# The feed-forward's first product from half-size products: seven in place of eight

## The chip, the cores and the metric

One core of a Trainium2 chip runs the whole program. The metric is the device time of one execution in microseconds (us). A core has a matrix engine (TensorE, PE in the profile, its weight loads PEld), a vector engine (VectorE, DVE), an activation engine (ScalarE, ACT), a general engine (GpSimd, POOL) and SyncE (SP), whose queue starts the loads. Every engine works through its own instructions in order and waits on semaphores for the others.

## The reference

A decoder layer over 512 tokens of 1024 features: a mixer of three head groups, its output projection, then a gated feed-forward with 2816 inner features. In float32:

```
h = rmsnorm(x, pre_mix_g[l])
proj = h @ w_in[l]
...
mix = jnp.concatenate([a_out, b_out, c_out], axis=-1) @ w_out[l]
x = x + rmsnorm(mix, post_mix_g[l])
h = rmsnorm(x, pre_ffn_g[l])
gate, up = jnp.split(h @ w_ffn_in[l], 2, axis=-1)
f = (jax.nn.silu(gate) * up) @ w_ffn_out[l]
x = x + rmsnorm(f, post_ffn_g[l])
```

The change is in `h @ w_ffn_in`: 512 x 1024 times 1024 x 5632.

## The kernel before, in words

Every large product is made of float32r matmuls in two parts. A factor is split into a high part (a cast to float32r, ScalarE, L183) and a low part (the rest, `wl = wf - wh`, VectorE or GpSimd, L185), and a product is high times high, high times low and low times high: three matmuls in place of one. Weights come as tiles of 128 x 1024 float32 (512 KB) in two raw buffers (`wf`, loaded by SyncE in `w_load`, L156), and go split into four pairs of buffers (`wh`, `wl`). `Feed` hands them out in the order of use, at a high priority.

TensorE's order is written by hand: a class `Order` keeps a clock of TensorE's work, runs one main sequence and slots in side sequences when what they wait for should be there. The order on the other engines is set by a scheduler from priorities, and their queues are then fixed.

Stages: the input norm and projection with the three mixers beside it; the output projection (`tm_gemm`, tokens on the partitions, 512 columns at a time); the norm of its result, turned by TensorE so that features lie on the partitions (`turn`, L1142 to L1156: `h2` and `l2`, high and low part, 128 x 8 x 512); then the feed-forward's first product. It has 22 blocks of 128 inner features. A block takes two weight tiles, gate and up columns, and makes two PSUM banks (128 features x 512 tokens) with 24 matmuls each (`ffn_mm`: eight depth blocks by three matmuls). Blocks 0 and 1 run in two halves of 256 tokens, since the second half of the tokens is turned later; blocks 2 to 21 with 512 columns. After a block `gate` applies silu on ScalarE (L1177), multiplies on VectorE (L1178) and splits the result for the second product (L1179, L1180). Banks alternate: `acc` (two) for even blocks, `sb` (three) for odd ones. The second product (`tm_gemm` again, with `w_ffn_out`) and the last norm end the program.

Of the kernel before, what the change touches and what calls it, by code (L numbers as in the profile page):

```python
# [96 lines left out]
def block_kernel(ctx: ExitStack, tc: tile.TileContext, x, pre_mix_g, w_in, rwkv_mu, rwkv_w0, rwkv_w2,  # L97
# [924 lines left out]
    def pair_slice(k):  # L1022
        return slice(k[0], k[1] + 1, k[1] - k[0])
# [22 lines left out]
    for ui, unit in enumerate(o_units):  # L1046
        if ui == 2:
# [4 lines left out]
            grow = early.tile([128, D], F32, name="grow")  # L1052
            frow = early.tile([128, D], F32, name="frow")
# [12 lines left out]
    wsp2 = ph2.enter_context(tc.tile_pool(name="wsplit2", bufs=2, side="right"))  # L1066

# [1 line left out]
    res = ph2.enter_context(tc.tile_pool(name="res", bufs=1))  # L1069
    wpools = (wspool, wsp2)  # L1070
    h2 = res.tile([128, KB, S], F32R, name="h2")
    l2 = res.tile([128, KB, S], F32R, name="l2")
    sm = res.tile([128, 3 * NB], F32, name="sm")
# [64 lines left out]
    def turn(t):  # L1138
        """The normed input of the feed-forward, features on the partitions."""
# [10 lines left out]
        for i in range(2):  # L1150
# [4 lines left out]
            act.copy(h2[:, 4 * i:4 * i + 4, tk], p3)  # L1155
            dve.tensor_tensor(l2[:, 4 * i:4 * i + 4, tk], p3, h2[:, 4 * i:4 * i + 4, tk].bitcast(F32), op=OP.subtract)  # L1156
# [11 lines left out]
    FM = FB - KB  # L1168
    fhm = res.tile([128, FM, S], F32R, name="fhm")
    flm = res.tile([128, FM, S], F32R, name="flm")  # L1170
    fh = [fhm[:, i] if i < FM else mh[:, i - FM] for i in range(FB)]
    fl = [flm[:, i] if i < FM else ml[:, i - FM] for i in range(FB)]
    ffeed = Feed([(w_ffn_in[0], slice(0, 8), c + 128 * b, 128) for b in range(FB) for c in (0, FF)], wpools, on_pool=(1, 3))

    def gate(b, pg):
        f = res.tile([128, S], F32, name="etmp", bufs=2)
        act.activation(f, pg[0], AF.Silu)  # L1177
        dve.tensor_tensor(f, f, pg[1], op=OP.mult)  # L1178
        act.copy(fh[b], f)  # L1179
        dve.tensor_tensor(fl[b], f, fh[b].bitcast(F32), op=OP.subtract)  # L1180
# [11 lines left out]
    ws = [ffn_w() for _ in range(4)]  # L1192
# [5 lines left out]
    gate(0, pf[0:2])  # L1198
    gate(1, pf[2:4])
    for b in range(2, FB):  # L1200
        pg = []
        for i in range(2):
            p = (sb if b % 2 else acc)()
            ffn_mm(p, *ffn_w(), slice(0, S))
            pg.append(p)
        gate(b, pg)
# [40 lines left out]
```

## Time and profile before

| what | us |
|---|---|
| three runs, median (lowest to highest) | 704.51 (702.69 to 706.77) |
| the profiled execution: span, first to last instruction | 700.0 |
| the profiled execution: its own time | not listed apart from the three runs |
| TensorE busy in the span | 671.8 |
| VectorE busy | 335.0 |
| ScalarE busy | 253.7 |
| GpSimd busy | 132.7 |
| blocks 2 to 21 of the first product, 351.7 to 570.4 | 218.7 |
| second product and end, 570.4 to 700.0 | 129.6 |

The profile is one execution. Busy time counts an instruction from its start to its end; TensorE's matmuls overlap (a new one starts before the last has ended), so the pace is read from one start to the next. A note in brackets behind a row gives the idle time ahead of it and who ended it. `x3` behind a row means three such instructions in a row, with their time from the first's start to the last's end.

### The profile page before, as it was taken

What the parts mean: (1) busy time and instruction counts of PE and PEld (TensorE: products, weight loads), DVE (VectorE), ACT (ScalarE), POOL (GpSimd) and SP (SyncE); (2) the same over time, 40 slices, a digit from 0 to 9 for tenths busy, and PEclk for the clock granted to TensorE, in tenths of its full rate; (3) what the DMA queues carried; (4) which work ended last, traced back from release to release, by engine and by line L of the source; (5) the groups of instructions that cost most, each with busy time, mean ns of one, the idle gap of its engine ahead of it and who ended that gap; (6) DMA issues with size and microseconds to landing.
All of it is one profiled execution on the core that took longest, in us unless ns stands there. A gap on an engine that the chain in (4) does not pass through costs nothing.

```text
span 700.0 us, 9724 instructions
## 1 busy us (share of the span) xinstructions
PE 671.8 (96%) x3918; PEld 546.1 (78%) x3918; DVE 335.0 (48%) x588; ACT 253.7 (36%) x451; POOL 132.7 (19%) x149
## 2 busy tenths in 40 slices
PE   7998999799999997998999999999999999999996
PEld 6876878577777785777988888888888888888885
DVE  4688879935353566458442332323323232223214
ACT  6753443335455454336332322233222331122111
POOL 6272435522413226115000000000000000000001
PEclk9999999799999998999999999999999999999999
DMA  7322112211101117233243333333333332223203
GB/s 238 113 62 61 45 43 69 86 32 34 52 31 31 31 61 247 83 92 116 67 139 101 90 91 94 109 100 90 91 94 109 99 90 91 91 91 100 99 13 121
DMA packets 80286, 61.15 MB, mean 87 GB/s; under 512 B 2120, under 2 KB 70128, under 8 KB 80240
## 3 DMA queue, kind: packets, MB, share of 16 engines
q1 hardware_dynamic: 78192, 57.70, 26.9%
q10 hardware_dynamic: 2048, 2.82, 1.2%
q8 instruction: 31, 0.51, 0.3%
q14 instruction: 15, 0.12, 0.1%
HBM read 58.41 MB, written 2.10 MB: 86 GB/s over the span
## 4 chain that ended last, share of the span: by engine, by line
PE 50%; DVE 2%; issue 1%; ACT 1%; POOL 1%; DVEq 0%; POOLq 0%; ACTq 0%
PE sb L112 21%; PE acc L112 21%; PE yb L112 3%; PE rb L112 3%; PE ob L112 2%; DVE x L1129 1%; DVE xs L1146 1%; ACT raw L1142 1%; POOL rs L1126 0%; POOL ss L1144 0%; DVE etmp L1116 0%; ACT wdad L1110 0%; DVE wl L185 0%; DVEq L1243 0%; PE rb L117 0%
## 5 line engine op out<-in xcount | busy, mean ns | idle before, releaser
L183 ACT ACTIVATE wh<-wf 128x1024 fp32r<-128x1024 f32 (+2 forms) x120 | 104.1, 886 | 285.6 <-PE sb L112 123.1
L185 DVE TENSOR_TENSOR wl<-wf,wh 128x1024 fp32r<-128x1024 f32 (+1 forms) x76 | 89.4, 1180 | 170.9 <-ACT wh L183 168.6
L185 POOL TENSOR_TENSOR wl<-wf,wh 128x512 fp32r<-128x512 f32 (+2 forms) x44 | 71.3, 1639 | 111.5 <-ACT wh L183 72.1
L1126 POOL TENSOR_TENSOR rs<-rs,mhalf 128x1 f32<-128x1 f32 x8 | 6.2, 778 | 380.0 <-DVE rs L1121 376.8
L112 PE MATMUL acc<-l,wh 128*128 128x512 f32 (+1 forms) x192 | 72.5, 378 | 1.9 <-DVE l L1156 1.9
L112 PE MATMUL acc<-h,wh 128*128 128x512 f32 (+1 forms) x192 | 72.2, 376 | 0.0
L112 PE MATMUL acc<-h,wl 128*128 128x512 f32 (+1 forms) x192 | 71.9, 374 | 0.0
L112 PE MATMUL sb<-l,wh 128*128 128x512 f32 (+1 forms) x192 | 71.6, 373 | 0.0
L112 PE MATMUL sb<-h,wh 128*128 128x512 f32 (+1 forms) x192 | 71.5, 373 | 0.0
L112 PE MATMUL sb<-h,wl 128*128 128x512 f32 (+1 forms) x192 | 71.1, 370 | 0.0
L112 PE MATMUL acc<-bigh,wh 128*128 128x512 f32 (+1 forms) x168 | 68.7, 412 | 0.8 <-ACT bigh L276 0.5
L112 PE MATMUL acc<-bigl,wh 128*128 128x512 f32 (+1 forms) x168 | 64.0, 386 | 0.3
L112 PE MATMUL acc<-bigh,wl 128*128 128x512 f32 (+1 forms) x168 | 59.6, 379 | 0.0
L112 PEld LDWEIGHTS acc<-l,wh 128*128 128x128 f32 x192 | 36.8, 192 | 8.3 <-DVE l L1156 2.2
L112 PEld LDWEIGHTS acc<-h,wh 128*128 128x128 f32 x192 | 36.8, 192 | 6.6
L112 PEld LDWEIGHTS acc<-h,wl 128*128 128x128 f32 x192 | 36.9, 192 | 6.5
L112 PEld LDWEIGHTS sb<-h,wh 128*128 128x128 f32 x192 | 36.1, 188 | 6.6
L112 PEld LDWEIGHTS sb<-h,wl 128*128 128x128 f32 x192 | 36.1, 188 | 6.5
L112 PEld LDWEIGHTS sb<-l,wh 128*128 128x128 f32 x192 | 36.1, 188 | 6.1
L112 PEld LDWEIGHTS acc<-bigh,wh 128*128 128x128 f32 x168 | 32.0, 190 | 9.3 <-issue 2.7
L112 PEld LDWEIGHTS acc<-bigl,wh 128*128 128x128 f32 x168 | 32.1, 191 | 5.6 <-DVE bigl L277 0.9
L112 PEld LDWEIGHTS acc<-bigh,wl 128*128 128x128 f32 x168 | 30.2, 191 | 6.3
(343 smaller groups left out, 1269.8 us busy)
## 6 DMA issues: line engine op xcount, KB each, us to landing
wf<-in_w_ffn_in_dram SPq DMA_DIRECT2D x44, 512.0 KB
wf<-in_w_ffn_out_dram SPq DMA_DIRECT2D x22, 512.0 KB
wf<-in_w_in_dram SPq DMA_DIRECT2D x21, 512.0 KB
wf<-in_w_out_dram SPq DMA_DIRECT2D x8, 512.0 KB
xt<-in_x_dram SPq DMA_DIRECT2D x4, 512.0 KB
x<-in_x_dram SPq DMA_DIRECT2D x4, 512.0 KB
out_dram<-x SPq DMA_DIRECT2D x8, 256.0 KB
wf<-in_w_in_dram SPq DMA_DIRECT2D x4, 384.0 KB
```

The source lines that it names most:

```text
L112: return nc.tensor.matmul(out_, lhsT, rhs, **kw)
L183: act.activation(h[:, c], t[:, c], AF.Copy)
L185: eng.tensor_tensor(l[:, c], t[:, c], h[:, c].bitcast(F32), op=OP.subtract)
L1126: pool.tensor_tensor(r, r, mhalf[:, 0:1], op=OP.pow)
L1129: dve.scalar_tensor_tensor(x2[:, t, c:d], src, r, x2[:, t, c:d], op0=OP.mult, op1=OP.add)
L1142: act.activation(raw[:, t, :].bitcast(BF), x2[:, t, :], AF.Square, scale=1.0 / 32, accum_out=ss[:, t:t + 1])
L1146: dve.scalar_tensor_tensor(xs, x2[:, t, :], ss[:, t:t + 1], frow, op0=OP.mult, op1=OP.mult)
```

## The change

Blocks 2 to 21 no longer multiply each weight tile with all tokens. The stacked gate and up columns (2 x 128 features), the depth (2 x 512) and the tokens (2 x 256) are halved, and the 2 x 2 by 2 x 2 product of quarters is made with seven products of quarters in place of eight, by the scheme with 15 additions. Weight quarters are `a11`, `a12` (gate), `a21`, `a22` (up); input quarters `b11` to `b22`.

- The input sums are made once (`t1` to `t4`, L1225 to L1232), from an unsplit copy `ht` of the turned input that `turn` now keeps (a second ScalarE copy of each piece, L1170), and split.
- Per block, four weight sums are made before splitting, in two tiles: `sa` (a21 + a22 on GpSimd L1274; that less a11 on VectorE L1275) and `sc` (a11 - a21 on GpSimd L1279; a12 less the first half of `sa` on VectorE L1280). `in_parts` splits (ScalarE L1262; low part L1263): a11 and a22 with GpSimd, `sa`, `sc` (1024 columns) and a12 with VectorE.
- `product` is twelve matmuls of 256 columns into the first half of a bank. The seven go into four banks, two of them used twice more (`first=False`): a11, s2, s1, a22, then s3 on top of s2's, s4 on top of s1's, a12 on top of a11's. Between the two uses a bank is read: `s1`, `s5` on ScalarE (L1307, L1313), `u2`, `u3` on VectorE (L1310, L1317).
- The sums of the results: `u2`, `u3`, `m`, `e` (VectorE, reading PSUM; half of `m` on GpSimd, L1319), then silu and the gate's product as before.
- Buffers: raw tiles are three (two of `wpool`, every third in the new pool `ffn`), and so are the wide split pairs; `sh`, `sl` are four; `sa`, `sc`, `s1`, `u2`, `u3`, `s5` have one each. Blocks 8 to 21 leave their result unsplit (`fr`) and it is split after the last block (L1349, L1350). Pools are closed and opened so that all fits.

```
+    def raw_tile(c0):
+        n_raw[0] += 1
+        t = (fp_ if n_raw[0] % 3 == 0 else wpool).tile([128, 1024], F32, name="wf")
...
+    def in_parts(src, eng):
+        h, l = parts(src.shape[1])
+        act.activation(h, src, AF.Copy)
+        eng.tensor_tensor(l, src, h.bitcast(F32), op=OP.subtract)
...
+    def weights(b):
...
+        g, u = raw_tile(128 * b), raw_tile(FF + 128 * b)
+        a11, a12, a21, a22 = g[:, :512], g[:, 512:], u[:, :512], u[:, 512:]
+        w = {}
+        w["a11"], = in_parts(a11, pool)
+        sa = fp_.tile([128, 1024], F32, name="sa")
+        pool.tensor_tensor(sa[:, 512:], a21, a22, op=OP.add)
+        dve.tensor_tensor(sa[:, :512], sa[:, 512:], a11, op=OP.subtract)
+        w["s2"], w["s1"] = in_parts(sa, dve)
+        w["a22"], = in_parts(a22, pool)
+        sc = fp_.tile([128, 1024], F32, name="sc")
+        pool.tensor_tensor(sc[:, :512], a11, a21, op=OP.subtract)
+        dve.tensor_tensor(sc[:, 512:], a12, sa[:, :512], op=OP.subtract)
+        w["s3"], w["s4"] = in_parts(sc, dve)
+        w["a12"], = in_parts(a12, dve)
+        return w
...
+    def product(p, w, x, first=True):
...
+        (wh, wl), (xh, xl) = w, BT[x]
+        p = p[:, :256]
+        for k in range(4):
+            pe.matmul(p, wh[:, k], xh[:, k], start=(first and k == 0), stop=False, skip_group_check=True)
+            pe.matmul(p, wh[:, k], xl[:, k], start=False, stop=False, skip_group_check=True)
+            pe.matmul(p, wl[:, k], xh[:, k], start=False, stop=(k == 3), skip_group_check=True)
...
+    for b in range(NPLAIN, FB):
+        with tc.high_priority(offset=PRI_W):
+            w = weights(b)
+        pa, (pb, pc, pd) = acc(), ((sb(), sb(), sb()) if b % 2 else (rb(), yb(), ob()))
...
+        product(pa, w["a11"], "b11")
+        with tc.high_priority(offset=2 * PRI_W):
+            act.copy(s1, qa)
+        product(pb, w["s2"], "t2")
+        with tc.high_priority(offset=2 * PRI_W):
+            dve.tensor_tensor(u2, qb, s1, op=OP.add)
+        product(pc, w["s1"], "t1")
+        with tc.high_priority(offset=2 * PRI_W):
+            act.copy(s5, qc)
+        product(pd, w["a22"], "t4")
+        product(pb, w["s3"], "t3", first=False)
+        with tc.high_priority(offset=2 * PRI_W):
+            dve.tensor_tensor(u3, qb, s1, op=OP.add)
+            dve.tensor_tensor(m[:, 0:256], u3, qd, op=OP.subtract)
+            pool.tensor_tensor(m[:, 256:512], u3, s5, op=OP.add)
+        product(pc, w["s4"], "b22", first=False)
+        with tc.high_priority(offset=2 * PRI_W):
+            dve.tensor_tensor(e[:, 256:512], qc, u2, op=OP.add)
+            act.activation(e[:, 256:512], e[:, 256:512], AF.Silu)
+        product(pa, w["a12"], "b21", first=False)
+        with tc.high_priority(offset=2 * PRI_W):
+            act.activation(e[:, 0:256], qa, AF.Silu)
```

VectorE in the middle of the stage, before: one weight split and one piece of the gate in turn (numbers tell tiles apart).

```order
L185 TENSOR_TENSOR wl_4035<-wf_4032,wh_4034 128x1024
L1180 TENSOR_TENSOR flm_3200<-etmp_3928,fhm_3199 128x512
L185 TENSOR_TENSOR wl_4071<-wf_4068,wh_4070 128x1024
L1178 TENSOR_TENSOR etmp_3995<-etmp_3995,sb_3964 128x512
L185 TENSOR_TENSOR wl_4102<-wf_4099,wh_4101 128x1024
```

VectorE in the middle of the stage, with the change, one block's period: rows with `wf_5122` and higher numbers belong to the block after the one whose `u2_5023` and `u3_5024` are made.

```order
L1275 TENSOR_TENSOR sa_5130<-sa_5130,wf_5122 128x512
L1280 TENSOR_TENSOR sc_5141<-wf_5122,sa_5130 128x512
L1310 TENSOR_TENSOR u2_5023<-sb_5019,s1_5022 128x256
L1263 TENSOR_TENSOR wl_5134<-sa_5130,wh_5133 128x1024
L1263 TENSOR_TENSOR wl_5145<-sc_5141,wh_5144 128x1024
L1263 TENSOR_TENSOR sl_5149<-wf_5122,sh_5148 128x512
L1317 TENSOR_TENSOR u3_5024<-sb_5019,s1_5022 128x256
```

The next block's two sums now stand ahead of this block's `u2`, and its three splits ahead of `u3`. GpSimd, which had no row in this stage, has five a block, here of the block that starts with `wf_5524` (gate) and `wf_5526` (up), and the half of `m` of the block before:

```order
L1274 TENSOR_TENSOR sa_5532<-wf_5526 128x512
L1279 TENSOR_TENSOR sc_5543<-wf_5524,wf_5526 128x512
L1263 TENSOR_TENSOR sl_5529<-wf_5524,sh_5528 128x512
L1263 TENSOR_TENSOR sl_5540<-wf_5526,sh_5539 128x512
L1319 TENSOR_TENSOR m_5429<-u3_5426,s5_5427 128x256
```

SyncE's loads with what they wait for (`DVE`, `Pool`: the last reader of the buffer; 4182/4184, 4318/4320, 4452/4454, 4586/4588, 4720/4722 are gate and up tiles of five blocks in turn). Before, a load there always waited for VectorE's L185.

```order
L1256 DMA wf_4184<-in_w_ffn_in_dram 128x8x128 [waits DMAHW3_49,DVE_49]
L1256 DMA wf_4452<-in_w_ffn_in_dram 128x8x128 [waits DMAHW0_49,Pool_49]
L1256 DMA wf_4320<-in_w_ffn_in_dram 128x8x128 [waits DMAHW6_49,DVE_49]
L1256 DMA wf_4454<-in_w_ffn_in_dram 128x8x128 [waits DMAHW2_49,Pool_49]
L1256 DMA wf_4586<-in_w_ffn_in_dram 128x8x128 [waits DMAHW7_49,DVE_49]
L1256 DMA wf_4720<-in_w_ffn_in_dram 128x8x128 [waits DMAHW3_49,Pool_49]
L1256 DMA wf_4588<-in_w_ffn_in_dram 128x8x128 [waits DMAHW1_49,DVE_49]
```

Up tiles 4184, 4320 and 4588 wait for VectorE, 4454 for GpSimd: two of three wait for VectorE, and gate tiles go out up to two blocks ahead.

## Rows read from the trace of the kernel before

**Rows 1.** The page's head and its part 1: busy us, share, instructions.
```profile
span 700.0 us, 9724 instructions
PE 671.8 (96%) x3918; PEld 546.1 (78%) x3918; DVE 335.0 (48%) x588; ACT 253.7 (36%) x451; POOL 132.7 (19%) x149
```

**Rows 2.** Stages: length, busy us PE, PEld, DVE, ACT, POOL, PEclk, DMA, GB/s.
```profile
323.20:329.40 6.20, 4.32 (x23) 4.00 (x22) 5.61 (x8) 3.73 (x6) 3.10 (x5) 0.72 0.58 181
...
351.70:570.40 218.70, 218.70 (x963) 180.28 (x962) 75.30 (x81) 63.64 (x81) 0.00 (x0) 1.00 0.34 99
570.40:700.00 129.60, 123.29 (x595) 102.23 (x593) 35.96 (x43) 26.35 (x38) 2.16 (x4) 0.99 0.26 86
```

**Rows 3.** The chain of waits: start us, length us, what.
```profile
340.57 5.71 PE acc L112 x48
346.28 5.59 PE sb L112 x48
...
559.63 10.93 PE sb L112 x48
```

**Rows 4.** TensorE in order of time, 325.4 to 329.4: start us, length us.
```profile
325.40 0.39 PE L112 MATMUL acc<-l,wh 128*128 128x256 f32 x1 [1.88 <-DVE l L1156]
...
326.01 0.42 PE L112 MATMUL acc<-h,wl 128*128 128x256 f32 x1
326.23 0.42 PE L112 MATMUL acc<-h,wh 128*128 128x256 f32 x1
...
329.22 0.34 PE L112 MATMUL acc<-h,wl 128*128 128x256 f32 x1
```

**Rows 5.** Groups by form, whole span: busy us, mean ns, idle before.
```profile
L185 DVE TENSOR_TENSOR wl<-wf,wh 128x1024 fp32r<-128x1024 f32 x68 | 83.2, 1224 | 168.5 <-ACT wh L183 166.3
...
L183 ACT ACTIVATE wh<-wf 128x512 fp32r<-128x512 f32 x38 | 21.9, 623 | 25.2 <-PE acc L112 23.1 <-POOL hsel L381 1.6 <-issue 0.4
```

**Rows 6.** GpSimd and VectorE in order of time, in four stretches.
```profile
224.61 2.54 POOL L185 TENSOR_TENSOR wl<-wf,wh 128x512 fp32r<-128x512 f32 x2 [5.35 <-PE sb L112]
44.43 3.01 POOL L185 TENSOR_TENSOR wl<-wf,wh 128x512 fp32r<-128x512 f32 x2
44.39 0.75 DVE L561 SCALAR_TENSOR_TENSOR kn<-vt,cols,ob 128x512 f32<-128x512 f32 x1 [1.30 <-PE ob L117]
45.17 1.10 DVE L562 SCALAR_TENSOR_TENSOR ar<-kn,ep 128x512 f32<-128x512 f32 x1
46.86 1.12 DVE L563 SCALAR_TENSOR_TENSOR kn<-kn,en 128x512 f32<-128x512 f32 x1
321.11 2.43 POOL L185 TENSOR_TENSOR wl<-wf,wh 128x1024 fp32r<-128x1024 f32 x1
321.18 2.90 DVE L1129 SCALAR_TENSOR_TENSOR x<-raw,rs,x 128x512 f32<-128x512 f32 x1 [0.43 <-POOL rs L1126]
324.00 0.74 DVE L1129 SCALAR_TENSOR_TENSOR x<-etmp,rs,x 128x512 f32<-128x512 f32 x1
264.83 1.89 DVE L801 TENSOR_TENSOR bigl<-y,bigh 128x512 fp32r<-128x512 f32 x3
```

**Rows 7.** ScalarE, VectorE and SyncE's queue in order of time, 343 to 353.
```profile
343.42 1.06 ACT L183 ACTIVATE wh<-wf 128x1024 fp32r<-128x1024 f32 x1 [5.00 <-issue]
344.51 1.22 DVE L185 TENSOR_TENSOR wl<-wf,wh 128x1024 fp32r<-128x1024 f32 x1 [5.27 <-ACT wh L183]
345.76 0.37 SPq L156 DMA_DIRECT2D wf<-in_w_ffn_in_dram  x1
350.00 1.06 ACT L183 ACTIVATE wh<-wf 128x1024 fp32r<-128x1024 f32 x1 [2.15 <-DMA wf<-in_w_ffn_in_dram]
347.37 1.23 DVE L185 TENSOR_TENSOR wl<-wf,wh 128x1024 fp32r<-128x1024 f32 x1 [0.26 <-ACT wh L183]
352.65 1.06 ACT L183 ACTIVATE wh<-wf 128x1024 fp32r<-128x1024 f32 x1 [1.11 <-DMA wf<-in_w_ffn_in_dram]
352.24 0.68 DVE L1178 TENSOR_TENSOR etmp<-etmp,sb 128x512 f32<-128x512 f32 x1
```

More of the change, by code (lines that the diff above doesn't have):

```diff
@@ L1051, in block_kernel @@
             x2 = early.tile([128, NB, D], F32, name="x2")
-            grow = early.tile([128, D], F32, name="grow")
-            frow = early.tile([128, D], F32, name="frow")
+            gains = ExitStack()
+            gfp = gains.enter_context(tc.tile_pool(name="gains", bufs=1, side="right"))
+            grow = gfp.tile([128, D], F32, name="grow")
+            frow = gfp.tile([128, D], F32, name="frow")
             act.dma_start(grow, brow(post_mix_g[0], D))
@@ L1065, in block_kernel @@
     ph1.close()
[L1066 to L1073 removed]
+    more = ExitStack()
+    wsp2 = more.enter_context(tc.tile_pool(name="wsplit2", bufs=2, side="right"))
+    hps = ExitStack()
+    hp = hps.enter_context(tc.tile_pool(name="normed", bufs=1))
+    trans = ExitStack()
+    res = trans.enter_context(tc.tile_pool(name="res", bufs=1))
+    wpools = (wspool, wsp2)
+    h2 = hp.tile([128, KB, S], F32R, name="h2")
+    l2 = hp.tile([128, KB, S], F32R, name="l2")
+    th_ = hp.tile([128, 3, 4, 256], F32R, name="th")
+    tl_ = hp.tile([128, 3, 4, 256], F32R, name="tl")
+    sm = ct([128, 3 * NB], "sm")
     raw = res.tile([128, NB, 512], F32, name="raw")
+    ht = res.tile([128, KB, S], F32, name="ht")
+    t3 = res.tile([128, 4, 256], F32, name="t3")
     def tm_gemm(fd, ah, al, units, fin, by_token, banks, halves=(0, 1), parts=1):
@@ L1165, in block_kernel, with to_parts @@
     tm_gemm(ofeed, mhk, mlk, o_units, ofin, 4, {1: (sb, sb, sb, ob)}, (1,))
[L1168 to L1178, printed above, removed]
+    FM = KB
+    NPLAIN = 2
+    fh = [mh[:, i] for i in range(FM)]
+    fl = [ml[:, i] for i in range(FM)]
+    ffeed = Feed([(w_ffn_in[0], slice(0, 8), c + 128 * b, 128) for b in range(NPLAIN) for c in (0, FF)], wpools,
+                 on_pool=(1, 3))
+    def to_parts(b, f):
         act.copy(fh[b], f)
@@ L1190, in ffn_w @@
         return tuple(w.rearrange("p (k c) -> p k c", k=KB) for w in ffeed.next())
-    ws = [ffn_w() for _ in range(4)]
+    ws = [ffn_w() for _ in range(2 * NPLAIN)]
     pf = [acc(), acc(), sb(), sb()]
@@ L1197, in block_kernel @@
             ffn_mm(p, *w, slice(256 * th, 256 * th + 256))
[L1198 to L1206, printed above, removed]
+    for b in range(NPLAIN):
+        f = res.tile([128, S], F32, name="etmp", bufs=2)
+        act.activation(f, pf[2 * b], AF.Silu)
+        dve.tensor_tensor(f, f, pf[2 * b + 1], op=OP.mult)
+        to_parts(b, f)
@@ new lines, in block_kernel, with quarter @@
+    K_ = [slice(0, 4), slice(4, 8)]
+    TK = [slice(0, 256), slice(256, 512)]
+    def quarter(t, k, tk):
+        return t[:, K_[k], TK[tk]]
+    b11, b12, b21, b22 = [quarter(ht, k, t) for k in range(2) for t in range(2)]
+    with tc.high_priority(offset=PRI_W):
+        dve.tensor_tensor(t3, b22, b12, op=OP.subtract)
+        dve.tensor_tensor(b12, b12, b11, op=OP.subtract)
+        dve.tensor_tensor(b22, b22, b12, op=OP.subtract)
+        dve.tensor_tensor(b21, b22, b21, op=OP.subtract)
+        for src, h, l in ((b22, th_[:, 0], tl_[:, 0]), (b12, quarter(h2, 0, 1), quarter(l2, 0, 1)),
+                          (b21, th_[:, 2], tl_[:, 2]), (t3, th_[:, 1], tl_[:, 1])):
+            act.copy(h, src)
+            dve.tensor_tensor(l, src, h.bitcast(F32), op=OP.subtract)
@@ new lines, in block_kernel @@
+    BT = {"b11": (quarter(h2, 0, 0), quarter(l2, 0, 0)), "b21": (quarter(h2, 1, 0), quarter(l2, 1, 0)),
+          "b22": (quarter(h2, 1, 1), quarter(l2, 1, 1)), "t1": (quarter(h2, 0, 1), quarter(l2, 0, 1)),
+          "t2": (th_[:, 0], tl_[:, 0]), "t3": (th_[:, 1], tl_[:, 1]), "t4": (th_[:, 2], tl_[:, 2])}
+    trans.close()
+    more.close()
+    gains.close()
+    ffs = ExitStack()
+    fr = ph2.enter_context(tc.tile_pool(name="inner", bufs=1, side="right")).tile([128, FB - FM, S], F32, name="fr")
@@ L1208, in block_kernel @@
+    ffs.close()
+    hps.close()
+    wsp2 = ph2.enter_context(tc.tile_pool(name="wsplit3", bufs=2, reuse_waits="tile"))
+    wpools = (wspool, wsp2)
+    fo = ph2.enter_context(tc.tile_pool(name="out", bufs=1, reuse_waits="tile"))
     f_units = [(k, k + 1) for k in range(0, FB, 2)]
-    orow = early.tile([128, D], F32, name="grow")
+    orow = fo.tile([128, D], F32, name="grow")
+    pools["raw"] = fo.tile([128, NB, 512], F32, name="raw")
+    pools["tmp"] = fo
     act.dma_start(orow, brow(post_ffn_g[0], D))
+    fhm = fo.tile([128, FB - FM, S], F32R, name="fhm")
@@ L1211, in block_kernel @@
+    flm = fo.tile([128, FB - FM, S], F32R, name="flm")
+    for b in range(FM, FB):
+        fh.append(fhm[:, b - FM])
+        fl.append(flm[:, b - FM])
+        act.copy(fh[b], fr[:, b - FM])
+        dve.tensor_tensor(fl[b], fr[:, b - FM], fh[b].bitcast(F32), op=OP.subtract)
     wfeed = Feed([(w_ffn_out[0], pair_slice(k), 512 * hf, 512) for hf in range(2) for k in f_units], wpools)
```

35 lines of the change are left out of this document (32 added, 3 removed).

## The prediction, made before the changed kernel was run

> **What bounds the kernel now.** I read the page's totals first, then the table by stages, the chain of waits inside the feed-forward stage, and last single rows of the engines. The page shows TensorE busy for 671.8 us of a span of 700.0, VectorE for 335.0, GpSimd for 132.7 [rows 1]. The stages say where the change falls: from 351.7 to 570.4 us the twenty blocks that it touches run, 218.7 us in which TensorE never rests, VectorE is busy for 75.3 us and GpSimd does nothing at all [rows 2]. The chain of waits there is matmuls alone: two products of 24 matmuls in 10.93 us, block after block [rows 3], so 0.228 us from one 512-column matmul to the next. TensorE bounds this stage and each block costs 10.93 us. The stretch just ahead of it has the same products in halves of 256 columns: 48 in 5.71 us and 48 in 5.59 [rows 3], 0.1165 to 0.119 us each, so half the columns cost a little over half the time, weight loads included.
>
> The times are three runs with a median of 704.51 us; the span of the profiled execution is 700.0 us. I work out a change of the span and add it to the median.
>
> **What TensorE gains.** A block goes from 48 matmuls of 512 columns to 84 of 256 (seven products, four depth blocks, three matmuls each). At 0.1165 to 0.119 us that is 9.8 to 10.0 us against 10.93: 0.9 to 1.1 us less a block, 19 to 23 us over twenty, if TensorE still is what everything waits for. The order of its instructions has 720 rows more, which is 20 times 84 less 48, so the change does what it says.
>
> **What the other engines get.** Per block, VectorE had two weight splits of 1.22 us [rows 5] and two pieces of the gate. Now GpSimd has four pieces of 512 columns (two sums of weight quarters, two splits) and one of 256; VectorE has two sums of 512, two splits of 1024, one of 512, four pieces of 256 that read PSUM, the gate's product and, in six blocks, one split more. ScalarE's two pieces of 1024 columns and seven of at most 512 (1.06 and 0.62 us [rows 5, 7]) are at most 6.5 us a block and stay hidden.
>
> GpSimd's 512-column piece takes 1.27 us where nothing disturbs it, two in 2.54 [rows 6]. The same pair beside VectorE took 3.01 us: in that time VectorE's piece with one input from PSUM ran at its usual 0.75, but the two pieces with both inputs in SBUF (L562, L563) took 1.10 and 1.12. The clearest case is at 321.11: GpSimd works for 2.43 us, VectorE's piece issued at 321.18 takes 2.90 and its twin right behind 0.74 [rows 6]. So a VectorE piece with two SBUF inputs and a GpSimd piece never run together; the later one waits for the whole other. Every GpSimd piece of the change is of that kind, and all VectorE pieces but the four that read PSUM. They must be added, not laid beside each other. A VectorE piece of 512 columns holds 0.60 us (three in a row take 1.89 [rows 6], the last of them 0.69), one of 1024 about 1.14 (1.22 less the same overlap).
>
> How much does a hand-over cost? The disturbed pair is longer by 3.01 - 2.54 = 0.47 us, and the VectorE piece that got in between holds 0.60, so the hand-over itself costs nothing; I take zero. The Trainium skill, "SBUF — State Buffer", section "A bandwidth-pool intuition that's wrong (but worth ruling out)", lets the loser go on only some 115 ns after the other's end. By that, eight hand-overs would add 0.9 us to a block and 18 us to the sum below, some 763 us; this trace does not show it.
>
> **The ring that closes.** In the new order VectorE's row for the next block's first weight sum (L1275) stands ahead of u2 (L1310) of the block that TensorE is in, and the fifth product, which goes on in the bank that u2 reads, cannot start before u2. That sum needs GpSimd's sum (L1274), which needs the second weight tile ("u"). In two blocks of three the load of u waits on VectorE: it gets the buffer that the block before frees with its last split (a12, L1263), since there are three raw buffers and a block takes two. In the third it waits on GpSimd. So once a block this is run through in series:
> - the load: VectorE's end at 344.51 + 1.22 = 345.73, issue at 345.76, first use at 350.00, 4.27 us; the next one 348.60 to 352.65, 4.05 us [rows 7]. I take 4.17. Nothing that needs both engines can fill it, for GpSimd's queue stands at the sum that waits for this load;
> - GpSimd's four pieces, 4 x 1.27 = 5.08;
> - VectorE's two sums and the a12 split, 3 x 0.60, and two splits of 1024, 2 x 1.14: 4.08. u2 itself lies beside GpSimd's last split.
>
> That is 13.33 us. In every third block the load goes out ahead of the last three VectorE pieces, 2.88 us earlier: 10.45. The mean is (2 x 13.33 + 10.45) / 3 = 12.37. Some ten steps from engine to engine at 0.03 us (ScalarE's end at 343.42 + 1.06 = 344.48, VectorE's start at 344.51 [rows 7]) make 12.7. The low bound is 12.0 (loads of 4.05 and a GpSimd piece that lets go 0.1 us early, as the 0.47 allows); the high one 13.8 (the two loads of 512 KB go out close together and the second is late by up to a microsecond). I take 12.7, as the rows have it. TensorE's 9.8 us fit inside, with one gap of 2.5 to 4 us a block, ahead of the fifth product. What it gains is then worth nothing, and twenty blocks cost 20 x (12.7 - 10.93) = **35.3 us** more.
>
> **The way in.** The last plain product ends at 351.7. The first block's first split (ScalarE) stands behind the second plain block's gate: VectorE's L1178 ends at 352.92 [rows 7], two ScalarE pieces of 0.62 follow [rows 5], then GpSimd's 1.27: 355.4. If GpSimd's piece has to wait for a VectorE one and that for it, 356.6. I take 4.3 us of TensorE idle, with 3.7 and 5.5 as bounds; before, there was none. Ahead of that, eight more ScalarE copies of 512 columns (0.62 each [rows 5]) lie in the turning of the normed input; two stand ahead of a copy that TensorE waits for at 325.40 [rows 4]: 0.7 us (0 to 1.2). The subtractions that make the input sums lie under the plain products. The way out costs nothing: splits of the inner features are fourteen pieces of 0.69 on VectorE, in a stage that leaves it idle for 94 of 130 us [rows 2], and the first four units of the last product do not need them.
>
> **Sum**: 35.3 + 4.3 + 0.7 = 40.3 us, span 740, time 704.5 + 40.3 = **745 us**, with bounds of 728 and 768.
>
> **Rivals.**
> - *The pair of engines is full, but the loads are in time* (704 us). If the ring does not close (a load is issued earlier than I read, or u2 gets ahead), what is left is the sum of the pieces that exclude each other: GpSimd 4 x 1.27 and about 0.70 for 256 columns, VectorE 4.08 and 0.60 for the gate's product: 10.46 us, in six blocks 0.60 more. 14 x 10.46 + 6 x 11.06 = 212.8 against 218.7, and 5.0 for the way in: 0.9 us less. For it: the two in three loads that wait on VectorE could land while GpSimd still has splits to do. Against: GpSimd's four pieces of a block all stand between two loads.
> - *TensorE keeps the bound* (689 us, faster). If pieces of VectorE and GpSimd ran side by side, GpSimd's 5.8 and VectorE's some 6 us both fit into 9.8 to 10.0, and loads in time give 20 x 9.9 = 198 against 218.7: 20.7 less, 5.0 back. It decides for this if the two-input VectorE pieces stay near 0.69 and 1.22 us in the stage. Against it stand the four stretched pieces [rows 6]. The Trainium skill, "TensorE: Matmul & The Clock Gate", section "Back-to-back issue gap", has 262 cycles for 256 columns, 109 ns: by that 9.2 us a block and 674 us; the rows have 0.1165 or more.
> - *The gaps cost clock as well* (774 us). After an idle stretch of 1.88 us the matmuls from 326.0 to 329.2 went 0.21 us apart instead of 0.118 [rows 4], at a granted clock of 0.72 for that stretch [rows 2]: the lower level for 15 matmuls, 1.45 us lost. A gap of 2.5 us or more in each block could do that twenty times: 29 us more. It decides once the slowed products run past the load that they wait beside; TensorE has 2.9 us of slack a block, so I expect most of it to be swallowed.
>
> **Chances.** Forecast 0.70; pair full 0.10; TensorE bound 0.07; clock as well 0.13. A measurement of this kernel tells some 0.5% (3.5 us) from no change. The second case spreads by some 8 us: 0.06 of it no change, 0.02 on either side. Faster 0.07 + 0.02 = 0.09, the same 0.06, slower 0.85. The range of 704 to 772 leaves out the fast case (0.07), some 0.04 of the second and half of the last, 0.17 in all.
>
> **What the next profile would show.** Right: in the block stage some 12.7 us a block; TensorE busy for about three quarters; one idle stretch a block whose releaser is VectorE's u2 (L1310); VectorE's L1275 and L1280 at 1.3 to 1.9 us instead of 0.69, and its own waits there put down to GpSimd's L1274. Wrong if L1280 is near 0.69 us, if the idle of TensorE there is under 0.5 us a block, or if it ends on something other than u2; the load's step is wrong if GpSimd's L1274 never waits for the transfer.

## The result, and the profile after

The changed kernel takes 744.42 us (median of 4 runs, 742.58 to 748.37); the kernel before took 703.6 us (702.03 to 706.77). The ratio is 1.058, with a 95% interval of 1.0533 to 1.0627: slower, at the forecast of 745. The profiled execution took 743.26 us, 41.5 us more in its span than the 700.0 of [rows 1].

The page's head and part 1 after the change; columns as in [rows 1].

```profile
span 741.5 us, 11709 instructions
...
PE 673.4 (91%) x4638; PEld 583.3 (79%) x4638; DVE 467.6 (63%) x736; ACT 309.2 (42%) x583; POOL 267.4 (36%) x249
```

GpSimd's busy time doubled (132.7 to 267.4), VectorE's rose by 132.6, TensorE's hardly moved. The places of the 41.5 us come from the chain of waits, pieces of four stages (start, length, what):

```profile
310.60 1.16 ACT raw L1155 x2
...
342.91 5.72 PE acc L112 x48
348.63 4.31 PE sb L112 x36
...
611.98 1.44 PE acc L112 x12
613.41 1.40 PE rb L112 x6
```

The first row is the turning of the normed input, which stood at 308.56 before: 2.04 us were lost ahead of the turn, where the edit only moves pools of memory. The four runs of the kernel before lie 4.7 us apart, so I take the 2 us as spread; no run shows it. The last plain products began at 340.57 before [rows 3] and 342.91 now, so the turn added only 0.3. They take some 11.3 us in both, and end at 351.87 and about 354.2. The block stage ends at 613.41; before it ended at 570.56, so its length went from 218.7 to 259.2, 40.5 us more. What follows it is 128.1 instead of 129.4. The sum is 2.0 + 0.3 + 40.5 - 1.3 = 41.5: nearly all of it lies in the stage.

That stage and the last product, by the table of stages; columns as in [rows 2].

```profile
354.20:613.40 259.20, 217.03 (x1683) 212.53 (x1682) 193.45 (x210) 106.29 (x188) 134.66 (x100) 0.95 0.29 84
613.40:741.50 128.10, 121.82 (x595) 102.33 (x593) 45.57 (x58) 34.22 (x53) 2.20 (x4) 0.99 0.29 99
```

TensorE stands idle for 42.2 us of a stage in which it never rested [rows 2]. Who ended that idle time, and what VectorE and GpSimd wait for, is in the list of waits of the stage (us in total, times, longest):

```profile
PE sb L112 <- DVE u L1310: 18.1, 9, 3.0
PE rb L112 <- DVE u L1310: 15.0, 9, 2.9
PE acc L112 <- ACT sh L1262: 3.6, 1, 3.6
PE acc L112 <- POOL sl L1263: 3.1, 1, 3.1
PE rb L112 <- DVE wl L1263: 1.5, 1, 1.5
...
POOL sa L1274 <- DMA wf<-in_w_ffn_in_dram: 35.7, 13, 3.3
...
DVE sa L1275 <- POOL sa L1274: 32.0, 19, 2.7
```

18 of the 20 blocks have one gap, up to 3.0 us, that ends with u2 (33.1 us in all, 1.8 each). It lies ahead of the fifth product, the first of three that use a bank a second time (the fifth s2's, the sixth s1's, the seventh a11's; the list of the change has two banks used twice more). VectorE's first sum waits for GpSimd's in 19 blocks, and GpSimd's waits for the load in 13. VectorE and GpSimd by form in the stage (busy us, mean ns, idle before); [rows 5, 6] answer to them:

```profile
L1263 DVE TENSOR_TENSOR wl<-sa,wh 128x1024 fp32r<-128x1024 f32 x20 | 37.9, 1897 | 0.0
L1275 DVE TENSOR_TENSOR sa<-sa,wf 128x512 f32<-128x512 f32 x20 | 35.3, 1764 | 32.0 <-POOL sa L1274 32.0
L1280 DVE TENSOR_TENSOR sc<-wf,sa 128x512 f32<-128x512 f32 x20 | 31.1, 1555 | 0.5
L1263 DVE TENSOR_TENSOR wl<-sc,wh 128x1024 fp32r<-128x1024 f32 x20 | 24.2, 1212 | 0.1
...
L1318 DVE TENSOR_TENSOR m<-u,ob 128x256 f32<-128x256 f32 x10 | 4.2, 421 | 0.3
...
L1263 POOL TENSOR_TENSOR sl<-wf,sh 128x512 fp32r<-128x512 f32 x40 | 68.7, 1731 | 3.5 <-POOL sl L1263 2.3 <-ACT sh L1262 1.2
L1279 POOL TENSOR_TENSOR sc<-wf 128x512 f32<-128x512 f32 x20 | 25.9, 1293 | 0.0
```

The sums take 1.76 and 1.56 us where a lone piece took 0.69 [rows 6]; the split that meets GpSimd takes 1.90, its twin behind it 1.21. GpSimd's own splits are stretched from 1.27 to 1.73 each. The piece that reads PSUM (L1318) stays at 0.42.

One run through the ring, from one load that ended the chain to the next:

```profile
452.81 3.88 DMA wf<-in_w_ffn_in_dram
...
456.83 1.30 POOL sa L1274
...
458.15 1.78 DVE sa L1275
...
461.54 0.42 DVE u L1310
...
463.76 1.21 DVE wl L1263
464.97 0.60 DVE sl L1263
...
465.60 3.75 DMA wf<-in_w_ffn_in_dram
```

From issue to issue it takes 12.79 us. At 461.54 u2 comes loose from behind the sums and TensorE's fifth product goes; VectorE works on at the first wide split (at 461.87, for 1.97 us), the second (463.76) and a12's (464.97), which frees the buffer that the next load takes.

The blocks are not alike. VectorE's a12 splits of three blocks on end:

```profile
501.59 0.68 DVE L1263 TENSOR_TENSOR sl<-wf,sh 128x512 fp32r<-128x512 f32 x1
...
514.56 0.68 DVE L1263 TENSOR_TENSOR sl<-wf,sh 128x512 fp32r<-128x512 f32 x1
...
525.44 0.68 DVE L1263 TENSOR_TENSOR sl<-wf,sh 128x512 fp32r<-128x512 f32 x1
```

From one to the next it takes 12.97 and 10.88 us, and then 13.19. In the two long ones GpSimd's sum waits for the load (3.01 and 2.60 us), in the short one it does not wait.

### The profile page after: what moved, and what is told of

It is laid out like the page before. It is cut to its first block, busy times and chain, and to the rows that moved or that the text cites. A ratio compares the mean times of both kernels' runs of the same rounds, so it can differ in the third digit from the quotient of the medians.

```text
span 741.5 us, 11709 instructions
## 1 busy us (share of the span) xinstructions
PE 673.4 (91%) x4638; PEld 583.3 (79%) x4638; DVE 467.6 (63%) x736; ACT 309.2 (42%) x583; POOL 267.4 (36%) x249
## 4 chain that ended last, share of the span: by engine, by line
PE 34%; DVE 8%; issue 6%; DMA 5%; POOL 3%; ACT 1%; POOLq 0%; DVEq 0%; ACTq 0%; SPq 0%
PE sb L112 11%; PE acc L112 10%; PE rb L112 5%; DMA wf<-in_w_ffn_in_dram 5%; PE yb L112 5%; PE ob L112 3%; POOL sa L1274 2%; DVE sa L1275 2%; DVE wl L1263 2%; DVE sl L1263 1%; DVE u L1310 1%; DVE sc L1280 1%; POOL sl L1263 0%; DVE bigl L1192 0%; DVE x L1142 0%
## 5 line engine op out<-in xcount | busy, mean ns | idle before, releaser
L185 POOL TENSOR_TENSOR wl<-wf,wh 128x512 fp32r<-128x512 f32 (+2 forms) x44 | 71.4, 1641 | 114.1 <-ACT wh L183 74.6
L183 ACT ACTIVATE wh<-wf 128x512 fp32r<-128x512 f32 (+2 forms) x80 | 61.5, 798 | 121.6 <-PE acc L112 36.1
L185 DVE TENSOR_TENSOR wl<-wf,wh 128x1024 fp32r<-128x1024 f32 (+1 forms) x36 | 40.2, 1129 | 77.4 <-ACT wh L183 77.2
L1263 POOL TENSOR_TENSOR sl<-wf,sh 128x512 fp32r<-128x512 f32 x40 | 68.7, 1731 | 3.5 <-POOL sl L1263 2.3
L1275 DVE TENSOR_TENSOR sa<-sa,wf 128x512 f32<-128x512 f32 x20 | 35.3, 1764 | 32.0 <-POOL sa L1274 32.0
L112 PE MATMUL acc<-h,sh 128*128 128x256 f32 x160 | 46.0, 287 | 3.6 <-ACT sh L1262 3.6
L112 PE MATMUL acc<-h,sl 128*128 128x256 f32 x160 | 46.0, 288 | 3.1 <-POOL sl L1263 3.1
L1274 POOL TENSOR_TENSOR sa<-wf 128x512 f32<-128x512 f32 x20 | 27.3, 1367 | 55.5 <-DMA wf<-in_w_ffn_in_dram 35.7
L1262 ACT ACTIVATE sh<-wf 128x512 fp32r<-128x512 f32 x60 | 37.4, 627 | 21.9 <-DMA wf<-in_w_ffn_in_dram 12.1
L112 PE MATMUL acc<-l,sh 128*128 128x256 f32 x160 | 45.8, 286 | 0.0
L1319 POOL TENSOR_TENSOR m<-u,s 128x256 f32<-128x256 f32 x20 | 14.8, 739 | 80.6 <-DVE u L1317 76.7
L1263 DVE TENSOR_TENSOR wl<-sa,wh 128x1024 fp32r<-128x1024 f32 x20 | 37.9, 1897 | 0.0
L1262 ACT ACTIVATE wh<-sa 128x1024 fp32r<-128x1024 f32 x20 | 21.2, 1058 | 38.3 <-DVE sa L1275 38.3
```

The source lines that it names most:

```text
L112: return nc.tensor.matmul(out_, lhsT, rhs, **kw)
L183: act.activation(h[:, c], t[:, c], AF.Copy)
L185: eng.tensor_tensor(l[:, c], t[:, c], h[:, c].bitcast(F32), op=OP.subtract)
L1262: act.activation(h, src, AF.Copy)
L1263: eng.tensor_tensor(l, src, h.bitcast(F32), op=OP.subtract)
L1274: pool.tensor_tensor(sa[:, 512:], a21, a22, op=OP.add)
```

## Experiments

The block time in each is the time from the first u2 to the last in the profiled execution, over 19. For the changed kernel (VectorE's rows of u2 in the stage: count, duration, first and last start) that is (606.3 - 370.9) / 19 = 12.39 us:

```profile
L1310 DVE TENSOR_TENSOR u<-rb,s x10: 408/410/411, 370.9 to 598.3; 128x256 f32<-128x256 f32 x10
L1310 DVE TENSOR_TENSOR u<-sb,s x10: 409/410/425, 384.4 to 606.3; 128x256 f32<-128x256 f32 x10
```

The last of the 19 intervals (598.3 to 606.3) is short, since no sums of a next block stand in it; without it the mean is 12.63. In no kernel does the last interval lower the mean by more than 0.25 us, so the column serves to compare them.

My theory: load, GpSimd's four pieces and VectorE's pieces, which exclude GpSimd's, run in one ring; TensorE's wait for u2 is where that shows. The rivals: u2's place in VectorE's queue is itself the cost; pieces do not exclude each other and the load alone is; or the load is not in the ring. Each experiment's ratio is to runs of the kernel before taken with it on the same chip (medians 702.5 to 704.6).

| kernel | median us | ratio to before, 95% | us a block |
|---|---|---|---|
| the change | 744.4 | 1.058 (1.0533 to 1.0627) | 12.39 |
| u2_first | 716.6 | 1.0217 (1.0154 to 1.028) | 11.36 |
| u2_alone | 740.6 | 1.0526 (1.0475 to 1.0577) | 12.45 |
| u2_s5 | 735.0 | 1.0426 (1.037 to 1.0483) | 12.08 |
| u2_back | 743.5 | 1.059 (1.0503 to 1.0677) | 12.29 |
| raw4_alone | 723.1 | 1.0275 (1.0219 to 1.0332) | 11.17 |
| raw4 | 707.9 | 1.0053 (1.0012 to 1.0095) | 10.51 |
| no_low | 705.7 | 1.003 (0.9989 to 1.0071) | 10.58 |
| dve_raw4 | 697.9 | 0.9954 (0.9922 to 0.9985) | 10.15 |
| all_dve | 695.8 | 0.9887 (0.9847 to 0.9926) | 10.06 |
| way_in | 691.2 | 0.9801 (0.9748 to 0.9854) | 10.21 |

**u2 ahead of the sums (u2_first).**

```diff
+        if u2 is not None:
+            dve.tensor_copy(sa[:, 0:1], u2[:, 0:1])
         dve.tensor_tensor(sa[:, :512], sa[:, 512:], a11, op=OP.subtract)
...
             dve.tensor_tensor(u2, qb, s1, op=OP.add)
+        if b + 1 < FB:
+            with tc.high_priority(offset=PRI_W):
+                wn = weights(b + 1, u2)
```

> Edit: VectorE's queue gets u2 of a block ahead of the two weight sums (L1275, L1280) of the next block, by a one-column copy of u2 into the sum's tile; nothing else moves. Theory (the ring of load, four GpSimd pieces and VectorE's pieces in series sets the 12.3 us a block; TensorE's wait for u2 is only where it shows): u2 comes early, TensorE's gap moves to the wait for a weight part (L1263) or a sum's part, the block stays at 12.0 to 12.6 us, time 744 (736 to 752). Rival (the place of u2 in VectorE's queue is what costs): the 33 us of TensorE's waits for u2 go, some 10.5 us a block, time 704 to 714.

Measured: 716.6 us, 11.36 us a block. My theory missed, and the rival's number nearly came. But "nothing else moves" was not so: the scheduler also put GpSimd's a11 split ahead of its sum in two blocks of three, where it fills the time of the load; ScalarE's s5 ahead of the casts of the next block's sums; and on VectorE the a12 split behind u3. (The expectation for u2_alone has the a12 split moved "ahead of e", but there it stood in the changed kernel too.) What moved the time had to be taken apart.

**u2 ahead and nothing else (u2_alone); u2 back, the rest kept (u2_back).** Edges between neighbours now hold every queue to a written order. In the notation of one queue, `s1`, `s4` are L1275, L1280, `lsa`, `lsc`, `l12` the splits, `c1`, `c5` ScalarE's copies s1 and s5, `g` the gate's product, and +1 marks the next block (VectorE in two blocks of three; in the third, g and lsa+1 also stand ahead of u2). In the kernels with held queues L1279, L1315 and L1318 are the former L1274, L1310 and L1313.

```diff
 u2_alone
-VectorE: s1+1 s4+1 u2 lsa+1 lsc+1 l12+1 u3 ma e g
+VectorE: u2 s1+1 s4+1 lsa+1 lsc+1 l12+1 u3 ma e g
-ScalarE, every third block: hsa+1 h22+1 c1
+ScalarE, every third block: c1 hsa+1 h22+1
 u2_back, against u2_first
-VectorE: u2 s1+1 s4+1 lsa+1 lsc+1 u3 l12+1 e ma g
+VectorE: s1+1 s4+1 u2 lsa+1 lsc+1 u3 l12+1 e ma g
```

> Edit: in VectorE's queue u2 of a block stands ahead of both weight sums of the next block, and ScalarE's copy s1, which u2 needs, ahead of the cast of those sums; every other row of VectorE, GpSimd, ScalarE and SyncE's queue is held in the changed kernel's order. The first kernel with u2 ahead had moved more (the a11 split on GpSimd ahead of L1274 in two blocks of three, the a12 split on VectorE ahead of e). Theory (ring of load, GpSimd's four pieces and VectorE's, u2's place only shows it): no gain, and since the sums and so the a12 split and its load now also wait for TensorE's second product, 12.3 to 13.5 us a block, time 740 to 768. Rival (u2 behind the sums is the cost): 704 to 720, as in the first kernel.

> Edit: the first kernel with u2 ahead (716.6 us), in all its orders, but u2 goes back behind both weight sums of the next block, and the one-column copy goes. Theory (what helped there was GpSimd's a11 split filling the load's time): stays at 11.3 to 11.8 us a block, time 712 to 730. Rival (u2's place is the cost): back to 12.3 us a block, 740 to 748.

Measured: 740.6 and 743.5 us. u2_alone falls as my theory has it; u2_back falls as the rival has it. Each half of the first edit alone is worth next to nothing (4 and 1 us), both together gave 28 us. The waits from 375 to 590 us, of u2_alone:

```profile
POOL sa L1279 <- DMA wf<-in_w_ffn_in_dram: 37.4, 12, 3.9
PE yb L112 <- ACT s L1318: 15.6, 8, 3.2
PE sb L112 <- ACT s L1318: 14.1, 9, 3.2
```

and of u2_back:

```profile
PE rb L112 <- DVE u L1315: 12.7, 6, 2.4
PE sb L112 <- DVE u L1315: 12.6, 7, 2.5
...
POOL sa L1279 <- DMA wf<-in_w_ffn_in_dram: 3.8, 5, 1.0
```

In u2_alone the load's wait stays whole, and TensorE waits as long as before, only for another row: s5, which ScalarE holds behind the casts of the next block's sums. In u2_back GpSimd no longer waits for the load (3.8 us; 32.8 in the changed kernel in these 215 us), and TensorE still waits for u2. So there are two closed paths: one of load, GpSimd and VectorE, without TensorE; and one through TensorE, whose rows u2 and s5 stand in order behind the next block's sums. In u2_back the a11 split that now stands ahead of GpSimd's sum ties it to TensorE: ScalarE's casts of single quarters wait 31.8 us there for products on `acc`, the split 20.4 us for those casts, and the sum stands behind it.

**s5 ahead too (u2_s5).**

```diff
-ScalarE: hsa+1 hsc+1 c5
+ScalarE: c5 hsa+1 hsc+1
```

> Edit: as the kernel with u2 ahead alone (740.6 us, 12.45 us a block), and ScalarE's copy s5, which TensorE waited for there (29.7 us in all, ahead of the sixth product), goes ahead of the casts of the next block's sums as well. Nothing that TensorE waits for on VectorE or ScalarE then stands behind the next block's sums; every other row is in the changed kernel's order. Theory (load, GpSimd's and VectorE's pieces run in a ring without TensorE): 12.2 to 12.6 us a block, time 736 to 746, TensorE's wait moves on to a weight part of the next block. Rival (rows that TensorE needs, queued behind the next block's sums, close the ring through TensorE): 11.2 to 11.5 us a block as in the first kernel with u2 ahead, 713 to 722.

Measured: 735.0 us, 12.08 us a block: a little under my range and far over the rival's. TensorE's wait did not go to a weight part, as I expected, but back to u2 (21.2 us from 375 to 590 us); u2 waited for s1, which ScalarE holds behind the cast of the up tile, and that waits for the load. GpSimd still waits for the load in 13 blocks (32.6 us): the path without TensorE gives the period, though the queues keep offering TensorE a new place to meet it. u2_first, which had s5 ahead as well, took 0.72 us a block less; the a11 split in the time of the load and the rest that the scheduler moved there are what is left for that, not taken apart further.

**A fourth raw buffer, in the changed kernel's order (raw4_alone) and with the order left to the scheduler (raw4).**

```diff
-        t = (fp_ if n_raw[0] % 3 == 0 else wpool).tile([128, 1024], F32, name="wf")
+        t = (wpool if n_raw[0] % 4 < 2 else fp_).tile([128, 1024], F32, name="wf", **({} if n_raw[0] % 4 < 2 else {"bufs": 2}))
...
-        e = fp_.tile([128, S], F32, name="e", bufs=2)
-        m = fp_.tile([128, S], F32, name="m", bufs=2)
+        e = fp_.tile([128, S], F32, name="e", bufs=1)
+        m = fp_.tile([128, S], F32, name="m", bufs=1)
```

> Edit: a fourth raw buffer (e and m with one buffer instead of two), with every row of VectorE, GpSimd and ScalarE in the changed kernel's order and the loads in the order of the blocks. u2 stays behind the sums. Theory (the load is 4.2 of the ring's 12.3 us in two blocks of three): 10.6 to 11.2 us a block, time 708 to 722. Rival (u2's place is the cost, whatever the loads do): 12 us or more, 738 or more.

> Edit: a fourth raw weight buffer, so that each block has its pair and a load no longer waits for the block just before it; to make room, e and m have one buffer instead of two. Theory (the load is a part of the ring, and out of it the pieces that exclude each other are left): 10.5 to 11.2 us a block, TensorE's waits for u2 nearly gone, GpSimd's L1274 no longer waits for a transfer, L1275 and L1280 still take 1.3 us or more; time 744 - 20 x 1.5 = 714 (705 to 722). Rival one (pieces do not exclude each other, the load alone was the cost): 10.1 us a block, TensorE full, time 700. Rival two (the load is not in the ring, engines alone set 12.3 us): no change, 744.

Measured: 723.1 us (11.17 us a block) and 707.9 us (10.51). The load was worth 1.22 us a block by itself, just inside the block time that I expected, and the time just outside its range; GpSimd's wait for it is gone in both. In raw4_alone, with u2 behind the sums, TensorE still waits for u2 (from 375 to 590 us):

```profile
PE sb L112 <- DVE u L1315: 8.6, 7, 2.3
PE rb L112 <- DVE u L1315: 7.9, 6, 2.3
```

How that path closes shows in VectorE's queue there:

```profile
464.39 1.61 DVE L1337 TENSOR_TENSOR fr<-e,m 128x512 f32<-128x512 f32 x1 [1.55 <-ACT e L1331]
465.93 1.78 DVE L1280 TENSOR_TENSOR sa<-sa,wf 128x512 f32<-128x512 f32 x1
```

The gate's product (L1337) waits for ScalarE's silu of the seventh product, and in two blocks of three it stands ahead of the next block's first sum (L1280), behind which the next u2 stands.

In raw4 the scheduler puts u2 ahead of L1275 (and L1280 behind the splits), those 16.5 us shrink to 3.2, and VectorE is busy for 136.5 of 150 us (400 to 550 us). Its rows of u2:

```profile
L1310 DVE TENSOR_TENSOR u<-rb,s x10: 409/411/413, 376.1 to 567.8; 128x256 f32<-128x256 f32 x10
L1310 DVE TENSOR_TENSOR u<-sb,s x10: 409/411/425, 387.2 to 575.8; 128x256 f32<-128x256 f32 x10
```

With both paths open the block takes 10.51 us, or (567.8 - 376.1) / 18 = 10.65 without the short last interval, in the slowest of the six runs (712.8 us). The full pair in the forecast's first rival has 212.8 us for twenty, 10.64.

**GpSimd's two splits left out (no_low).** The high parts stand in for the low ones, so the kernel leaves out part of the arithmetic of two products. The cut is against the changed kernel with its queues held.

```diff
         queue("h" + k, "ACT", b, act.activation(h, src, AF.Copy))
-        queue("l" + k, "DVE" if eng is dve else "POOL", b, eng.tensor_tensor(l, src, h.bitcast(F32), op=OP.subtract))
+        if eng is pool:
+            l = h
+        else:
+            queue("l" + k, "DVE" if eng is dve else "POOL", b, eng.tensor_tensor(l, src, h.bitcast(F32), op=OP.subtract))
```

> Edit: GpSimd's two splits of a block (low parts of a11 and a22) are left out, and the high part stands in for them; every remaining row keeps the changed kernel's order. Left out: part of the arithmetic of two of seven products. Theory (GpSimd's pieces hold VectorE off and lie in the ring): VectorE's L1280 and its first 1024-column split fall to 0.7 and 1.2 us, two pieces of 1.27 us or most of them leave the ring: 10.1 to 10.9 us a block, time 700 to 716. Rival (these pieces lie beside other work, the ring is load, sums and VectorE's splits): 12 us or more a block, 738 or more.

Measured: 705.7 us, 10.58 us a block, as the theory has it. VectorE by form in its stage (L1283, L1271 and L1288 are the former L1275, L1263 and L1280):

```profile
L1283 DVE TENSOR_TENSOR sa<-sa,wf 128x512 f32<-128x512 f32 x20 | 35.3, 1766 | 32.6 <-POOL sa L1282 32.6
L1271 DVE TENSOR_TENSOR wl<-sa,wh 128x1024 fp32r<-128x1024 f32 x20 | 24.4, 1222 | 0.7 <-ACT wh L1267 0.2
...
L1288 DVE TENSOR_TENSOR sc<-wf,sa 128x512 f32<-128x512 f32 x20 | 13.8, 689 | 0.5
```

The sum that still meets a GpSimd piece keeps 1.77 us; the two pieces whose GpSimd neighbour is gone fall to 0.69 and 1.22. Two pieces of 1.27 us were worth 1.81 us a block. That they lie beside other work is refuted.

**All pieces on VectorE (all_dve), and with four raw buffers (dve_raw4).**

```diff
-        w["a11"], = in_parts(a11, pool)
+        w["a11"], = in_parts(a11, dve)
...
-        pool.tensor_tensor(sa[:, 512:], a21, a22, op=OP.add)
+        dve.tensor_tensor(sa[:, 512:], a21, a22, op=OP.add)
...
-        w["a22"], = in_parts(a22, pool)
+        w["a22"], = in_parts(a22, dve)
...
-        pool.tensor_tensor(sc[:, :512], a11, a21, op=OP.subtract)
+        dve.tensor_tensor(sc[:, :512], a11, a21, op=OP.subtract)
...
-            pool.tensor_tensor(m[:, 256:512], u3, s5, op=OP.add)
+            dve.tensor_tensor(m[:, 256:512], u3, s5, op=OP.add)
```

> Edit: the four GpSimd pieces of a block's weights and its piece of m go to VectorE; three raw buffers as in the changed kernel. Theory (ring with the load still in it, pieces of 0.60 us instead of 1.27): L1275 and L1280 fall to 0.60 to 0.70 us; VectorE has some 9.1 us of work a block (9.7 in the first six) and, where the load waits for the a12 split, 4.2 us without work but for what stands between; 11 to 12.5 us a block, time 718 to 744, middle 732. Rival (GpSimd beside VectorE is the whole cost, loads are in time): TensorE full at 10.1 us a block, time 698.

> Both edits together: no GpSimd piece in the block stage, four raw buffers. Theory (ring open, no exclusion): VectorE's 9.1 to 9.7 us a block lie just under TensorE's 84 x 0.119 = 10.0; 10.0 to 10.4 us a block, TensorE's waits for u2 under 0.3 us a block; 744 - 20 x 2.1 = 702, and a way in shorter by one to three us: 700 (694 to 707), the same as the kernel before the change. Rival (VectorE then is the bound, with every wait on its own queue): 11 us a block or more, time 718 or more.

Measured: 695.8 and 697.9 us, TensorE full at 10.06 and 10.15 us a block. The second came as expected. The first did not: my theory had 718 to 744 us, and the rival's 698 nearly came; three buffers are enough. VectorE in order of time, from the a12 split that frees a buffer to the sum that needs the load:

```profile
473.04 0.69 DVE L1263 TENSOR_TENSOR sl<-wf,sh 128x512 fp32r<-128x512 f32 x1
473.64 0.42 DVE L1317 TENSOR_TENSOR u<-rb,s 128x256 f32<-128x256 f32 x1
473.98 1.22 DVE L1263 TENSOR_TENSOR wl<-sc,wh 128x1024 fp32r<-128x1024 f32 x1
...
476.84 0.69 DVE L1263 TENSOR_TENSOR sl<-wf,sh 128x512 fp32r<-128x512 f32 x1 [0.65 <-ACT sh L1262]
477.52 0.69 DVE L1274 TENSOR_TENSOR sa<-wf 128x512 f32<-128x512 f32 x1
```

Here 3.8 us lie between the two, all but 0.7 of them work that needs no new tile: about as long as a load (3.75 and 3.88 above). I had counted on much less there. The sums take 0.687 us in this kernel (L1275, L1280).

**Memory for the way in (way_in).** In all_dve TensorE still stands idle for 4.7 us behind the plain blocks: the first parts lie over the gates' tiles, which are read until 359.0. This kernel is all_dve with those tiles elsewhere.

```diff
-            return tuple(fp_.tile([128, 512], F32R, name=x, bufs=4) for x in ("sh", "sl"))
+            n_small[0] += 1
+            return tuple((hp if n_small[0] % 4 in (1, 2) else fp_).tile([128, 512], F32R, name=x, bufs=2)
+                         for x in ("sh", "sl"))
...
-        sa = fp_.tile([128, 1024], F32, name="sa")
+        sa = hp.tile([128, 1024], F32, name="sa")
```

> Edit: as all pieces on VectorE with three raw buffers (695.8 us), and two of the four pairs of buffers for 512-column parts and the tile of sums lie in the pool of the normed input, not over the tiles that the plain blocks' gates still read. Theory (the first block's first product waits 3.6 us for memory under those tiles, then 1.1 us more for parts, at 1.2 GHz after): TensorE's idle on the way in falls from 4.7 to 0 to 1.5 us, time 691 (688 to 694). Rival (VectorE is full on the way in, and the wait only moves to the fifth product): 694 to 697.

Measured: 691.2 us, ratio 0.9801: this version beats the kernel before and the change. Its interval overlaps that of all_dve, so what it gains on that one rests on the profiles (spans of 690.3 and 695.0 us). The stages of 10 us around the way in, of all_dve:

```profile
350.00:360.00 10.00, 6.38 (x53) 6.18 (x52) 7.03 (x9) 4.89 (x7) 0.00 (x0) 0.90 0.00 1
360.00:370.00 10.00, 8.91 (x46) 8.32 (x47) 9.80 (x16) 5.53 (x10) 0.00 (x0) 0.59 0.59 172
```

and of this kernel:

```profile
350.00:360.00 10.00, 10.00 (x86) 10.00 (x85) 7.96 (x10) 6.06 (x9) 0.00 (x0) 1.00 0.01 2
360.00:370.00 10.00, 9.20 (x73) 8.60 (x71) 8.43 (x15) 5.83 (x11) 0.00 (x0) 1.00 0.69 191
```

60 more matmuls fit into the same 20 us, partly by the idle time, partly by the granted clock, which now stays at 1.00. A part of the wait moved, as the rival has it: 2.7 us for VectorE's wide splits (L1265) between 350 and 400 us, where I expected at most 1.5.

## Why the prediction was right, and where not

- *TensorE's gain.* Nearly right, and worth nothing in the change. With TensorE full (all_dve) a block takes 10.06 us, 0.12 per matmul; the forecast had 9.8 to 10.0. The Trainium skill ("TensorE: Matmul & The Clock Gate", section "Back-to-back issue gap") has 262 cycles for 256 columns, an estimate of 9.2 us a block; no run here shows that.
- *Pieces exclude each other.* Shown: the sums at 1.76 and 1.56 us, 0.69 without GpSimd. L1275 beside GpSimd's 1.29 us takes 0.47 more than it, less than its own 0.60, so handing over costs nothing that could be measured. With the 115 ns of the Trainium skill ("SBUF — State Buffer", section "A bandwidth-pool intuition that's wrong (but worth ruling out)") the forecast's estimate was 763 us, and the trace does not agree.
- *The ring.* The sum for a block whose load waits for VectorE was 13.33 us, for the third block 10.45, with 0.3 for steps on top; from a12 split to a12 split the stretch shown above has 12.97 and 13.19, and 10.88. So both kinds of block are there, the long ones somewhat shorter than the sum, the short one about as it says. A run through the chain takes 12.79, with a load of 3.75 to 3.88 in place of 4.17. Over all blocks, from the first product at 357.96 to 613.41, a block takes 12.77; 3.1 us of that are a wait of the way in, and without it it is 12.62: 20 x (12.62 - 10.93) = 33.8 for the forecast's 35.3.
- *The way in* was sized too small. TensorE stood idle for 3.7 us ahead of the first product and, two matmuls later, for 3.1 more until GpSimd's first split: 6.8 us for the forecast's 4.3, which had that split in it, and above its bound of 5.5. The forecast had the split follow right behind the second plain block's gate. ScalarE's first split waited until 357.3 for VectorE's last row of that gate (L1192), and in GpSimd's queue two sums stand ahead of the split (357.38 to 359.88). The turn took 0.3 (0.7), the way out nothing.
- *Luck.* The blocks cost 1.5 us less than forecast and the way in 2.5 more. The 2.0 us ahead of the turn and the 1.3 behind the stage were in no term and nearly cancel. So 744.4 against 745 is closer than the terms are. The low bound, too, is 729.6 by its own terms (704.5 + 20 x 1.07 + 3.7), not 728.
- *The clock.* The stage was granted 0.95. Two products (24 matmuls, from 411.39) that followed a gap took 5.49 us in place of 2.88. TensorE is busy for 217.0 us, where 20 x 10.06 = 201 would do: for 84% of the stage, not the three quarters of the forecast, and its gaps are 1.8 us, not 2.5 to 4. The block time stayed near the ring's sum all the same, which speaks for the delays being mostly swallowed, as forecast; no run measures it by itself.
- *The step that failed* is a half-sentence of the first rival: if the ring does not close, "a load is issued earlier than I read, or u2 gets ahead", the full pair is left. The price was right (10.65 for 10.64), the "or" was not. u2 ahead alone left 12.45, the load out alone 11.17; only both give 10.51. The forecast drew one ring where there are two: with the load out the one through TensorE is left, about 1.2 us shorter, and with u2 ahead the one of the load, nearly as long as before.
- *What stays open.* No kernel frees TensorE of every row behind the next block's sums and leaves all else as in the change: u2_alone left s5 there, u2_s5 left s1 behind the cast of the up tile. That the period there is the other path's rests on the load's wait in their lists. And raw4 differs from raw4_alone in more rows than u2.

## What to carry to other kernels

A piece moved to an idle engine is not free when the two engines cannot run it side by side: here four pieces of 1.27 us on GpSimd stood in for pieces of 0.60 on VectorE and held VectorE off as well, and giving them back turned 6% slower into 1% faster. Before trusting a saving on the bounding engine, walk each closed path of queue, buffer and load, and expect several of similar length: opening one gains no more than its distance to the next (here u2 ahead alone gave 4 us, the load out alone 21, both 37). When an experiment moves one row, compare all queues: a scheduler may move others, and they may be what pays.

## Not expected of the hardware

That VectorE, with every piece of the stage in its queue, was busy for 136.0 of 150 us (400 to 550 us, all_dve) and did not slow TensorE, which ran at a granted clock of 1.00 there. And that the change of buffers for the way in was repaid twice: TensorE's idle fell from 4.7 to 2.7 us, and the stretch at a granted clock of 0.59 went with it.
